# Decoder step with PEER experts: the samples' depthwise convolution on GpSimd, a later place for the second dense group's transposes, and two tile places moved

## The chip, the cores and the metric

The kernel runs on one core of one Trainium2 chip. The metric is the device time of one execution in microseconds (us). In the text PE is TensorE, DVE is VectorE, ACT is ScalarE, POOL is GpSimd and SP is SyncE, which here only starts DMAs. L277 means line 277 of the kernel before, as the profile names it. In the changed kernel most lines from 418 to 736 stand one lower, those from 742 to 884 one higher and those behind up to three higher; the rows of its instruction order carry its own numbers.

## The reference

One layer of a hybrid decoder is applied to 512 prompt tokens and to 32 new tokens of eight sequences (four each, the samples). Each token (1024 values) is projected to retention (queries, keys, values, gate) and to a convolution branch. Retention keeps a 128 x 128 state for each head and sequence. The convolution branch is a gated linear unit and then a causal depthwise convolution over 31 taps, with the last 30 rows of a cache ahead of the samples:

```python
u = ca * jax.nn.sigmoid(cg)
xpad = jnp.concatenate([buf, u], axis=1)
y = conv(xpad, dw_kernel) + dw_bias          # 31 taps, each channel by itself
y = silu(layer_norm(y, ln_g, ln_b))
```

Both branches go through an output projection, are added to the input and normalized to x1. Then PEER: eight heads score x1's queries against two sets of 128 keys, take the best 16 of the sums, and so choose 16 of 16,384 experts for each head and token. Expert e adds `gate * gelu(u_e . x1) * v_e`. A last normalization gives the output. New states and caches are outputs too.

## The kernel before

The 544 tokens are four groups in the expert stage: the first 128 prompt tokens (x1_0, experts gathered by index tile I), the 32 samples (Is), 128 more prompt tokens (Ib), and 256 prompt tokens whose experts are computed densely: all 128 x 128 experts are multiplied with x1 (L884), and a sparse gate matrix is built to weight the products. Those 256 are two dense groups of 128 (`DG`).

The stages, by the profile's times: From 0 to 100 us the first 128 prompt tokens and the samples go through projection (L209), convolution, retention, output projection (L503) and normalization; for the samples the convolution `conv_s` is 62 instructions of 128 x 128 elements: L286 and L287 for the first tap and the bias, then a product into `tap_s` (L290) and an addition (L291) for each of 30 taps. From 91 to 111 the first queries are made (L209, copied by ACT's L753), scored (L545, copied by L547), and the best taken on DVE. From 111 on POOL issues gathers (L628, 1 MB each), and DVE works on each with L634 (dot product), ACT with L645 and L646 (gelu, gate), DVE with L651 (sum). This gather stream is woven into all that follows up to about 734.

From 130 to 412 the other 416 tokens go the same way. Half of their convolution is done on PE (L270) with diagonal matrices that ACT writes (L269); between them stands `retain_s`, the samples' retention: the states of two sequences at a time are loaded (L395), multiplied (L424), updated (L431 on PE, L433 on DVE) and written back (L437). The first pair has a place of its own, `states`, loaded in front on ACT's queue; pairs 2 and 4 lie in the two halves of the tile that also holds the keys; the last pair takes `states` again, loaded on SP's queue after the first has been written back. L785 copies the samples' convolution (`samples`) to the other tokens' (`blk`); L816 loads the samples' x into a place named `xr0`, which held the first tokens' x before.

From 413 to 650 queries, key scores and retrieval for the other groups run, with dense products L884 between them (`early_keys`). Then each dense group's indices are split into row and column numbers on DVE (L919 to L925), transposed by PE (L928), copied by ACT (L932 to L936) and split into two halves on DVE (L938, L940). With these `first_keys` builds gate rows from 684 to 912: M (L989) and B (L993) on DVE, A on ACT and DVE (L978, L985, L986), multiplied on PE (L1009), applied on DVE (L1038) and ACT. From 912 the second dense products (L1066), the last builds, the samples' and the third group's gathers and the end follow.

The order on each engine is set by a scheduler that plays the program through before it is built; `behind(a, b)` makes only the order (a is placed after b), `await_` a wait. Tiles come from pools; a tile that takes the place of another waits for the last use of that one. Each engine works its queue in order, and a waiting instruction holds all that stand behind it.

Of the kernel before, what the change touches and what calls it, by code (L numbers as in the profile page):

```python
# [21 lines left out]
D = 1024  # L22
# [16 lines left out]
FREE = 30  # L39
TB_AT = (30, 34, 56, 80)  # L40
SECOND = 34
TURN = 88
EG = (32, 20, 44, 32)
E0S = (0, 32, 52, 96)

# [53 lines left out]
def tile_step(ctx: ExitStack, tc: tile.TileContext, a, o):  # L99
# [180 lines left out]
    def conv_s(y, after):  # L280

        yp = y.rearrange("p m (b i) -> p m b i", b=SB)
        for k in range(CK):
            w = dw[:, :, k].unsqueeze(2).unsqueeze(3).to_broadcast([128, 4, SB, SQ])
            if k == 0:
                behind(V.tensor_tensor(yp, u_s[:, :, :, 0:SQ], w, op=OP.mult), after)  # L286
                V.tensor_tensor(y, y, dwb.unsqueeze(2).to_broadcast([128, 4, NS]), op=OP.add)  # L287
                continue
            t = small("tap_s", [128, 4, SB, SQ], bufs=1)
            V.tensor_tensor(t, u_s[:, :, :, k:k + SQ], w, op=OP.mult)  # L290
            V.tensor_add(yp, yp, t)  # L291

    def conv_norm(y, n):

# [99 lines left out]
    def load_states(b, r0, q=nc.scalar):  # L394
        return q.dma_start(r0, a["state_retention"][0, b:b + 2].rearrange("b h d e -> d b h e"))  # L395

    def retain_s(qT, kT, v, gT):
# [12 lines left out]
                     start=(h == 0), stop=False, skip_group_check=True)  # L410
        yield
        room = keys_or_scratch()
        rooms = [states, room[:, 0:D], room[:, D:], states]
        for b in range(0, SB, 2):
            r0 = rooms[b // 2].rearrange("p (b h e) -> p b h e", b=2, h=H)
            vx = [small("on", [128, 512]) for _ in range(2)]
            for j in range(2):
                S.activation(vx[j][:n], v[:n], AF.Copy, scale=cc("blk")[:n, b + j:b + j + 1])
            if b:
                load_states(b, r0, nc.sync)  # L420
            for h in range(H):
                for j in range(2):
                    cs = h * n + (b + j) * SQ
                    T.matmul(po[:, cs:cs + SQ], r0[:, j, h], qT[:, h, (b + j) * SQ:(b + j + 1) * SQ],  # L424
                             start=False, stop=(h == H - 1 and b + j == SB - 1), skip_group_check=True)
                if h % 2:
                    yield
            for h in range(H):
                pk = mmps()[:, 0:256]
                for j in range(2):  # L430
                    T.matmul(pk[:, j * DH:(j + 1) * DH], kt[:n, h * DH:(h + 1) * DH], vx[j][:n, h * DH:(h + 1) * DH],  # L431
                             start=True, stop=True)
                V.scalar_tensor_tensor(r0[:, :, h], r0[:, :, h], float(GAMMA[h] ** SQ),  # L433
                                       pk.rearrange("p (b e) -> p b e", b=2), op0=OP.mult, op1=OP.add)
                if h % 2:
                    yield
            nc.sync.dma_start(o[4][0, b:b + 2].rearrange("b h d e -> d b h e"), r0)  # L437
# [299 lines left out]

    advance(0, k_tokens(k0, 0, C, "p"), v0)
    states = fe.tile([128, D], F32, name="states")
    behind(load_states(0, states.rearrange("p (b h e) -> p b h e", b=2, h=H)), lastk)  # L740
    xT = per.tile([128, 8, n], F32, name="x1T")
    nc.scalar.dma_start(xT[:, :, NS:], xt_v[:, :, 160:])
    x1T, xT = xT, xT[:, :, NS:]
# [114 lines left out]
    left = ExitStack()  # L858
    rp = left.enter_context(tc.tile_pool(name="rp", bufs=1, reuse_waits="tile"))
    sel[0] = left.enter_context(tc.tile_pool(name="sel", bufs=2))  # L860
    leftp = ExitStack()
    pq = leftp.enter_context(tc.tile_pool(name="pq", bufs=4, space=PSUM, reuse_waits="tile"))
    psp = [leftp.enter_context(tc.tile_pool(name="psp", bufs=4, space=PSUM, reuse_waits="tile"))]

    banks[:] = [pq]
    load_keys(pool=rp)
    ln2 = [bc_row("lng", a["ln2_g"], D), bc_row("lnb", a["ln2_b"], D)]

    def places(e, ne):
# [20 lines left out]
    qs = {}  # L890
    q_at = lambda c0, w: lambda h, s: qs[h // 2][:, h % 2 * 2 + s, c0:c0 + w]
    DG = ((0, 128), (128, ND - 128))

    for h0 in range(0, PH, 2):
        w = load_w(a["w_query"], h0 * 256)
        qs[h0 // 2] = rp.tile([128, 4, n], F32, name="qs", bufs=2)
        for m in range(4):
            S.activation(qs[h0 // 2][:, m], project(w, m, x1T, 0, n), AF.Copy)
        for h in (h0, h0 + 1):
            key_scores([(h, lambda s: q_at(NS, 128)(h, s))], sb[:, h])  # L900
        p0 = h0 % 4 * NS
        key_scores([(h, lambda s, h=h: q_at(0, NS)(h, s)) for h in (h0, h0 + 1)], ss_[p0:p0 + 2 * NS, h0 // 4], p0)
        if h0 % 4:
            for g, (c0, m) in enumerate(DG):
                retrieve(fresh(q_at(NG2 + c0, m)), range(h0 - 2, h0 + 2), m, eg[:, g], eg[:, 2 + g], h0 - 2)
# [6 lines left out]
            S.activation(places(e, 2), sp, AF.Gelu)  # L912
        return mm

    turned = early_keys(E0S[2], TURN)
    for g, (c0, m) in enumerate(DG):
        ef = eg[:m, g].rearrange("p h k -> p (h k)")
        ei = rp.tile([128, 128], I32, name="ei")[:m]
# [7 lines left out]
        p = mmps().rearrange("p (q t) -> p q t", q=4)  # L926
        for q, t in enumerate((e1, e2, eg[:m, 2 + g].rearrange("p h k -> p (h k)"))):
            mm = T.transpose(p[:, q, :m], t, ident[:m, :m])  # L928
            if g == q == 0:
                behind(mm, turned)  # L930
        gr = rp.tile([128, 128], F32, name="e2")[:, :m]
        S.activation(gr, p[:, 2, :m], AF.Copy, scale=GS)  # L932
        cs = slice(c0, c0 + m)
# [12 lines left out]

    w_, r_ = GSP["s"]
    topk_of("s", lambda h: ss_[:, h], 0, PH // r_, 128)
    early_keys(TURN, E0S[3])
    gbs = ExitStack()  # L950
    gb = gbs.enter_context(tc.tile_pool(name="gb", bufs=1, side="right", reuse_waits="tile"))
    GW[0] = gb.tile([128, EG[0], ND], F32, name="Gb")
# [258 lines left out]
```

## Time and profile before

| | us |
|---|---|
| timed runs (three) | 1500.69, 1508.7, 1509.43; median 1508.7 |
| profiled execution | 1498.04 |
| its span on the core | 1496.3, granted clock 0.988 |
| PE busy | 1437.5 (96%) |
| DVE busy | 1206.1 (81%) |
| ACT busy | 486.6 (33%) |
| POOL busy | 410.3 (27%) |

How it is read: busy time counts an engine's instructions but not waiting and not the issue of DMAs by a queue. PE records twice each product of two float32 tiles. A row of the timeline gives start, length, engine, line and operation, what is written from what, sizes and, in brackets, the idle time ahead of it with what ended it; rows with a count are runs of the same instruction. The waits list, for an engine and line, which engine or DMA ended the idle time ahead of it: total, times, the longest. The chain is followed back from the last instruction to what released each step.

### The profile page before, as it was taken

What the parts mean: (1) busy time and instruction counts of PE and PEld (TensorE: products, weight loads), DVE (VectorE), ACT (ScalarE), POOL (GpSimd) and SP (SyncE); (2) the same over time, 40 slices, a digit from 0 to 9 for tenths busy, and PEclk for the clock granted to TensorE, in tenths of its full rate; (3) what the DMA queues carried; (4) which work ended last, traced back from release to release, by engine and by line L of the source; (5) the groups of instructions that cost most, each with busy time, mean ns of one, the idle gap of its engine ahead of it and who ended that gap; (6) DMA issues with size and microseconds to landing.
All of it is one profiled execution on the core that took longest, in us unless ns stands there. A gap on an engine that the chain in (4) does not pass through costs nothing.

```text
span 1496.3 us, 19303 instructions
## 1 busy us (share of the span) xinstructions
PE 1437.5 (96%) x6486; PEld 981.9 (66%) x6486; DVE 1206.1 (81%) x2977; ACT 486.6 (33%) x1492; POOL 410.3 (27%) x329
## 2 busy tenths in 40 slices
PE   8899989999999999989989999997999999999998
PEld 7877667567857678878878875443454666666443
DVE  4979899997747999998789997677989866666666
ACT  1424452345112322235445543112673111111110
POOL 1002534432323222222222220333333422222330
PEclk9999999999999999999999999998999999999999
DMA  9759678984799789999999985999899999999995
GB/s 345 296 196 409 227 269 280 390 340 155 289 401 369 253 295 348 338 345 355 315 355 343 336 293 173 345 423 416 336 370 391 409 412 410 410 402 406 409 415 194
DMA packets 99536, 503.60 MB, mean 337 GB/s; under 512 B 10183, under 2 KB 21191, under 8 KB 56549
## 3 DMA queue, kind: packets, MB, share of 16 engines
q0 software_dynamic: 42240, 305.12, 52.6%
q1 hardware_dynamic: 53197, 190.61, 33.8%
q10 hardware_dynamic: 4000, 6.64, 1.3%
q8 instruction: 51, 0.84, 0.2%
q14 instruction: 48, 0.39, 0.1%
HBM read 496.96 MB, written 5.80 MB: 336 GB/s over the span
## 4 chain that ended last, share of the span: by engine, by line
PE 40%; DVE 28%; DMA 21%; issue 9%; POOL 2%; ACT 1%; DVEq 0%; SPq 0%; POOLq 0%; ACTq 0%
PE pB L1066 17%; PE sp L884 14%; DMA g<-in_uv_dram,I 8%; DMA g<-in_uv_dram,Ib 7%; DVE acc L651 6%; DVE g L634 6%; DMA g<-in_uv_dram,Is 3%; PE mm L209 3%; POOL g L628 2%; DVE g L277 2%; PE mm L503 1%; PE mm L1009 1%; PE mm L270 1%; PE mm L318 1%; DVE iu L533 1%
## 5 line engine op out<-in xcount | busy, mean ns | idle before, releaser
L884 PE MATMUL sp<-x1T,uv 128*128 128x256 f32 x2048 | 464.1, 383 | 0.9 <-ACT Gc L1024 0.5
L634 DVE SCALAR_TENSOR_TENSOR g<-g,x 128x1024 f32<-128x1024 f32 x288 | 350.1, 1217 | 107.6 <-DMA g<-in_uv_dram,I 50.0
L884 PEld LDWEIGHTS sp<-x1T,uv 128*128 128x128 f32 x2048 | 385.8, 191 | 67.6 <-issue 14.0
L651 DVE SCALAR_TENSOR_TENSOR acc<-g,wgt,acc 128x1024 f32<-128x1024 f32 x285 | 364.2, 1278 | 66.3 <-ACT wgt L646 65.4
L628 POOL DMA_INDIRECT g<-in_uv_dram,I x128 | 185.5, 1449 | 423.2 <-DVE acc L651 242.3
L645 ACT ACTIVATE act<-act 128x1 f32<-128x1 f32 x288 | 58.0, 201 | 621.0 <-DVE g L634 620.6
L628 POOL DMA_INDIRECT g<-in_uv_dram,Ib x128 | 160.0, 1250 | 359.7 <-PE pB L1066 125.2
L209 PE MATMUL mm<-x1T,w 128*128 128x384 f32 (+1 forms) x512 | 177.0, 504 | 0.0
L1066 PE MATMUL pB<-uv,Ga 128*128 128x512 f32 x352 | 158.4, 596 | 0.0
L209 PEld LDWEIGHTS mm<-x1T,w 128*128 128x128 f32 x512 | 97.3, 192 | 72.8 <-issue 40.7
L1066 PEld LDWEIGHTS pB<-uv,Ga 128*128 128x128 f32 x352 | 65.7, 190 | 69.6 <-issue 66.5
L1066 PE MATMUL pB<-uv,Gb 128*128 128x512 f32 x256 | 111.4, 594 | 0.0
L1066 PE MATMUL pB<-uv,Gd 128*128 128x512 f32 x256 | 110.0, 592 | 0.0
L1066 PEld LDWEIGHTS pB<-uv,Gd 128*128 128x128 f32 x256 | 48.6, 190 | 60.8 <-issue 59.5
L1066 PEld LDWEIGHTS pB<-uv,Gb 128*128 128x128 f32 x256 | 48.2, 190 | 61.2 <-issue 55.7
L628 POOL DMA_INDIRECT g<-in_uv_dram,Is x32 | 41.3, 1289 | 149.0 <-DVE acc L651 30.9
L985 ACT ACTIVATE off<-row,e1T 128x128 bf16<-128x128 bf16 x256 | 78.9, 393 | 4.1 <-PE mm L1009 3.7
L1066 PE MATMUL pB<-uv,Gc 128*128 128x512 f32 x160 | 74.5, 611 | 0.7 <-DMA uv<-in_uv_dram 0.6
L1009 PEld LDWEIGHTS <-A 128*128 128x128 f16 x1024 | 43.4, 97 | 41.1 <-issue 22.4
L1022 ACT ACTIVATE W<-sp 128x256 f32<-128x256 f32 (+26 forms) x84 | 26.8, 319 | 124.1 <-PE sp L884 106.5
L209 PE MATMUL mm<-g,w 128*128 128x160 f32 (+1 forms) x512 | 65.4, 287 | 0.0
L209 PEld LDWEIGHTS mm<-g,w 128*128 128x128 f32 x512 | 64.4, 191 | 0.7
(287 smaller groups left out, 1595.3 us busy)
## 6 DMA issues: line engine op xcount, KB each, us to landing
uv<-in_ut_dram SPq DMA_DIRECT2D x128, 512.0 KB
uv<-in_uv_dram SPq DMA_DIRECT2D x128, 512.0 KB
w<-in_w_in_dram SPq DMA_DIRECT2D x18, 1024.0 KB
w<-in_w_query_dram SPq DMA_DIRECT2D x16, 1024.0 KB
w<-in_w_out_dram SPq DMA_DIRECT2D x7, 1024.0 KB
g<-in_uv_dram,I POOLq DMA_INDIRECT x128, 8.4
g<-in_uv_dram,Ib POOLq DMA_INDIRECT x128, 9.6
x1T<-in_xT_dram ACTq DMA_DIRECT2D x1, 1536.0 KB
```

Source lines behind the costliest of these rows:

```text
L209: T.matmul(p[:, :n], w[m // 2][:, k, (m % 2) * 128:(m % 2 + 1) * 128], xT[:, k, c0:c0 + n], start=(k == 0), stop=(k == 7))
L270: T.matmul(p[:, :L], dg[:, k % 4], u_p[:, m, p0 + k:p0 + k + L], start=(k == 0), stop=(k == CK - 1))
L277: V.scalar_tensor_tensor(y[:, m], u_p[:, m, p0 + k:p0 + k + L], dw[:, m, k:k + 1], y[:, m], op0=OP.mult, op1=OP.add)
L628: fetch = G.indirect_dma_start(out=t, out_offset=None, in_=a["uv"], in_offset=bass.IndirectOffsetOnAxis(ap=idx[:, k:k + 1], axis=0))
L634: dot = V.scalar_tensor_tensor(t[:, :D], t[:, :D], 1.0, x1, op0=OP.mult, op1=OP.mult, accum_out=act[:, 0:1])
L645: S.activation(act[:, 1:2], act[:, 0:1], AF.Gelu)
L651: V.scalar_tensor_tensor(acc, v, wgt, acc, op0=OP.mult, op1=OP.add)
L884: mm = T.matmul(sp[:, i], u[:, k], x1T[:, k, NG2:], start=(k == 0), stop=(k == 7), skip_group_check=True)
L985: S.activation(off[:, t], row, AF.Abs, bias=e1T[:, t1 + t:t1 + t + 1])
L1009: mm = T.matmul(pt[:, t % nt], A[t % TB], B[:, q, t % TB // 2, :, t % 2], start=(q == 0), stop=(q == 1))
L1022: S.activation(W[:, :n], sp[:, :n], AF.Gelu)
L1066: return [T.matmul(pB[b][q], W[:, b * 128:(b + 1) * 128], vt[:, q * 512:(q + 1) * 512], start=False, stop=(e == NK - 1), skip_group_check= ...
```

## The change

There are four edits.

1. `conv_s` issues all its 62 instructions on POOL (`G`) instead of DVE (`V`).
2. `early_keys` for keys 52 up to 94 is called twice ahead of the dense groups: up to 88 and from 88 to 94. The first transpose of group 0 is ordered behind the first call, that of group 1 behind the second. Before, one call went up to 88, group 1's had no order of its own, and the rest of the keys up to 96 came later.
3. `retain_s` takes the pairs in the order 0, 6, 2, 4. Pair 6 has a place `states6`, a tile named `xr0`, loaded in front on ACT's queue with pair 0; only 2 and 4 are loaded by SP inside the loop.
4. The queries of the other groups (`qs`) and the keys lie in a new pool `rk`, opened after the retrieval's `sel`, and the first `qs` is placed ahead of the keys. So the build rows, whose tiles come after this region is closed, lie over queries and keys and no longer over the retrieval's tiles.

```diff
-TURN = 88
+TURN = (88, 94)
...
     def conv_s(y, after):
...
-                behind(V.tensor_tensor(yp, u_s[:, :, :, 0:SQ], w, op=OP.mult), after)
-                V.tensor_tensor(y, y, dwb.unsqueeze(2).to_broadcast([128, 4, NS]), op=OP.add)
+                behind(G.tensor_tensor(yp, u_s[:, :, :, 0:SQ], w, op=OP.mult), after)
+                G.tensor_tensor(y, y, dwb.unsqueeze(2).to_broadcast([128, 4, NS]), op=OP.add)
...
-            V.tensor_tensor(t, u_s[:, :, :, k:k + SQ], w, op=OP.mult)
-            V.tensor_add(yp, yp, t)
+            G.tensor_tensor(t, u_s[:, :, :, k:k + SQ], w, op=OP.mult)
+            G.tensor_add(yp, yp, t)
...
-        rooms = [states, room[:, 0:D], room[:, D:], states]
-        for b in range(0, SB, 2):
-            r0 = rooms[b // 2].rearrange("p (b h e) -> p b h e", b=2, h=H)
+        for b, place in ((0, states), (6, states6), (2, room[:, 0:D]), (4, room[:, D:])):
+            r0 = place.rearrange("p (b h e) -> p b h e", b=2, h=H)
...
-            if b:
+            if b in (2, 4):
                 load_states(b, r0, nc.sync)
...
-    behind(load_states(0, states.rearrange("p (b h e) -> p b h e", b=2, h=H)), lastk)
+    states6 = fe.tile([128, D], F32, name="xr0")
+    for b, place in ((0, states), (6, states6)):
+        behind(load_states(b, place.rearrange("p (b h e) -> p b h e", b=2, h=H)), lastk)
...
+    rk = left.enter_context(tc.tile_pool(name="rk", bufs=1, reuse_waits="tile"))
...
-    load_keys(pool=rp)
...
+    qs[0] = rk.tile([128, 4, n], F32, name="qs", bufs=2)
+    load_keys(pool=rk)
...
-        qs[h0 // 2] = rp.tile([128, 4, n], F32, name="qs", bufs=2)
+        qs[h0 // 2] = qs[0] if h0 == 0 else rk.tile([128, 4, n], F32, name="qs", bufs=2)
...
-    turned = early_keys(E0S[2], TURN)
+    turned = [early_keys(*x) for x in ((E0S[2], TURN[0]), TURN)]
...
-            if g == q == 0:
-                behind(mm, turned)
+            if q == 0:
+                behind(mm, turned[g])
...
-    early_keys(TURN, E0S[3])
+    early_keys(TURN[1], E0S[3])
```

**POOL, at about 67 to 111 us.** Before, POOL did only two reciprocal roots here, each an addition (L194) and a power (L195): `hrs` for the heads' normalization, `lrs` for the layer normalization that gives x1_0. Then come the gathers.

```order
L194 TENSOR_SCALAR hrs_621<-hrs_621 128x4 [waits DVE_49]
L195 TENSOR_TENSOR hrs_621<-hrs_621,mhalf_102 128x4 [waits Pool_49]
L194 TENSOR_SCALAR lrs_717<-lmv_713 128x1 [waits DVE_49]
L195 TENSOR_TENSOR lrs_717<-lrs_717,mhalf_102 128x1 [waits Pool_49]
L628 DMA g_2581<-in_uv_dram,I0_114 128x2048 [waits DVE_49,DMASW0_49,PE_49,Activation_49]
```

In the changed kernel one product (L290) stands ahead of the loads in front, 41 of the convolution's instructions stand between `hrs` and `lrs`, and one more inside `lrs`:

```order
L291 TENSOR_TENSOR samples_127<-samples_127,tap_s_1314 128x128 [waits Pool_49]
L290 TENSOR_TENSOR tap_s_1317<-u_s_108,cols_90 128x128 [waits Pool_49]
L291 TENSOR_TENSOR samples_127<-samples_127,tap_s_1317 128x128 [waits Pool_49]
L194 TENSOR_SCALAR lrs_717<-lmv_713 128x1 [waits DVE_49]
L290 TENSOR_TENSOR tap_s_1320<-u_s_108,cols_90 128x128 [waits Pool_49]
L195 TENSOR_TENSOR lrs_717<-lrs_717,mhalf_102 128x1 [waits Pool_49]
L291 TENSOR_TENSOR samples_127<-samples_127,tap_s_1320 128x128 [waits Pool_49]
```

Behind these stand 18 more and then the gathers. Each waits for POOL's one before. On ACT the copy of the result (L785) keeps its place between the first and the second copy of the first queries (L753), and waits for POOL's last convolution instruction instead of DVE's.

**ACT, at about 211 to 223 us.** The rows are diagonals for PE (L269), a gather's gelu and gate (L644 and L645 there, L645 and L646 before), and the load of the samples' x, which before stood in front at 85.5 us, where the load of pair 6 now stands.

```order
L269 ACTIVATE dg<-cst_89,cols 128x128 [waits PE_49]
L269 ACTIVATE dg<-cst_89,cols 128x128 x3
L817 DMA xr_2268<-in_x_dram 32x1024 [waits DMAHW5_49,DMAHW4_49,DVE_49]
L644 ACTIVATE act<-act 128x1 [waits DVE_49]
L645 ACTIVATE wgt<-act,GT_113 128x1 [waits Activation_49]
L269 ACTIVATE dg<-cst_89,cols 128x128 [waits PE_49]
```

The load now waits for the write-back of pair 6 from the same place (DMAHW4), which SP issues after the pair's last update on DVE.

**PE, at about 650 to 684 us.** Dense products (L884) around the transposes of the second dense group (L928), before:

```order
L884 MATMUL sp<-x1T,uv 128x256 x2
L928 MATMUL mm<-cst_89,e_4129 128x128 [waits DVE_49]
L884 MATMUL sp<-x1T,uv 128x256 x5
L884 MATMUL sp<-x1T,uv 128x256 [waits DMAHW6_49]
L884 MATMUL sp<-x1T,uv 128x256 x4
L928 MATMUL mm<-cst_89,e_4131 128x128 [waits DVE_49]
L928 MATMUL mm<-cst_89,eg 128x128
```

In the changed kernel, where the two lines are L885 and L931:

```order
L885 MATMUL sp<-x1T,uv 128x256 [waits DMAHW0_49]
L885 MATMUL sp<-x1T,uv 128x256 x7
L931 MATMUL mm<-cst_89,e_4199 128x128 [waits DVE_49]
L931 MATMUL mm<-cst_89,e_4201 128x128 [waits DVE_49]
L931 MATMUL mm<-cst_89,eg 128x128
L885 MATMUL sp<-x1T,uv 128x256 [waits DMAHW1_49,Activation_49]
```

From the first group's transposes to the second group's first one stand 19 products before and 48 now; 16 follow up to the first L1009 now, 37 before.

More of the change, by code (lines that the diff above doesn't have):

```diff
@@ L424, in retain_s @@
                     T.matmul(po[:, cs:cs + SQ], r0[:, j, h], qT[:, h, (b + j) * SQ:(b + j + 1) * SQ],
-                             start=False, stop=(h == H - 1 and b + j == SB - 1), skip_group_check=True)
+                             start=False, stop=(h == H - 1 and b + j == 5), skip_group_check=True)
                 if h % 2:
```

## The prediction

> **What bounds the kernel now.** I read the page's head first, then PE's waits, then the timelines at the places that the change touches. Start with the busy times.
>
> ```profile
> span 1496.3 us, 19303 instructions
> PE 1437.5 (96%) x6486; PEld 981.9 (66%) x6486; DVE 1206.1 (81%) x2977; ACT 486.6 (33%) x1492; POOL 410.3 (27%) x329
> ```
>
> PE is busy in all but 58.8 us of the span, so a gain must come out of those 58.8, and every new stall of PE is lost time unless DVE would have stopped PE a little later anyway. PE's waits, longest first (us in total, times, longest):
>
> ```profile
> PE mm L1009 <- DVE Ga L1038: 8.9, 7, 1.7
> PE mm L1009 <- DVE B L993: 8.9, 2, 6.3
> ...
> PE mm L928 <- DVE e L922: 6.6, 1, 6.6
> ...
> PE mm L424 <- DMA states<-in_state_retention_dram: 2.7, 1, 2.7
> ```
>
> The change aims at two of these rows: 6.6 (second dense group's transposes) and 2.7 (last states). The rest, the two DVE rows of L1009 above all, is not touched directly. The profiled execution took 1498.04 us, 1.7 more than its span. The three timed runs have a median of 1508.7, so the span is 0.8% below it; my sum is a difference against the profiled execution, carried over to the runs at the end.
>
> **The samples' convolution on POOL.** First what its 62 instructions cost on DVE and whether they are in anyone's way there (count, busy us, mean ns):
>
> ```profile
> L291 DVE TENSOR_TENSOR samples<-samples,tap_s 128x128 f32<-128x128 f32 x30 | 8.7, 291 | 0.9
> L290 DVE TENSOR_TENSOR tap_s<-u_s,cols 128x128 f32<-128x128 f32 x30 | 8.7, 290 | 0.8
> L532 DVE MAX8 vf<-score 128x8 f32<-128x128 f32 x4 | 1.0, 282 | 5.6 <-ACT score L547 5.6
> ```
>
> With L286 and L287 that is 18 us, but after it DVE stands still for 5.6 us until a score arrives, and DVE's path instructions in this stretch begin when PE releases them:
>
> ```profile
> 82.85 1.89 PE L503 MATMUL mm<-w,g 128*128 128x256 f32 x8
> 84.78 0.69 DVE L732 SCALAR_TENSOR_TENSOR x<-xr,mm 128x512 f32<-128x512 f32 x1
> 88.15 3.62 PE L318 MATMUL mm<-x1T,g 128*32 128x256 f32 x16
> 88.23 1.41 DVE L485 SCALAR_TENSOR_TENSOR x<-x,lrs,lnb 128x512 f32<-128x512 f32 x2
> 91.70 0.66 PE L514 MATMUL mm<-cst,x 128*128 128x128 f32 x4
> ```
>
> L732 starts 0.04 after L503's end; L485 ends at 89.64, and its reader L514 waits for PE's own L318 until 91.70. So I put the 18 us freed on DVE at nothing: PE's L503 and L318 hide them.
>
> On POOL the same instructions are a chain, each waiting for the one before, and two things now stand behind them: the second normalization's rsqrt (lrs) behind 41 of them, and ACT's L785 behind all 61 that come after hrs. POOL's rows, from the timeline, from the groups (mean ns of one behind the bar), and of L195 all lrs together (minimum/median/maximum ns):
>
> ```profile
> 67.39 0.23 POOL L194 TENSOR_SCALAR hrs<-hrs 128x4 f32<-128x4 f32 x1 [15.29 <-DVE hrs L335]
> 67.71 1.06 POOL L195 TENSOR_TENSOR hrs<-hrs,mhalf 128x4 f32<-128x4 f32 x1
> 86.67 0.23 POOL L194 TENSOR_SCALAR lrs<-lmv 128x1 f32<-128x1 f32 x1 [17.90 <-DVE lmv L472]
> 86.98 0.90 POOL L195 TENSOR_TENSOR lrs<-lrs,mhalf 128x1 f32<-128x1 f32 x1
> ...
> L201 POOL MEMSET u_p<- 128x120 f32 x1 | 0.2, 190 | 0.0
> L188 POOL MEMSET mhalf<- 128x1 f32 x1 | 0.1, 90 | 0.0
> ...
> L195 POOL TENSOR_TENSOR lrs<-lrs,mhalf x7: 568/584/1562, 87.0 to 938.1; 128x1 f32<-128x1 f32 x5, 32x1 f32<-32x1 f32 x2
> ```
>
> A 128x128 tensor_tensor on POOL is not in the trace. Bounds for the step d from one to the next, with the 0.08 us that lie between dependent POOL rows (67.62 to 67.71): not under 0.23 + 0.08 = 0.31, the smallest arithmetic row; not over 1.06 + 0.08 = 1.14, four elements of a power. I take the plain L194, since mult and add are plain, and add the length: the memset grows by 0.10 us from 1 to 120 elements, and two inputs and an output are three such streams: 0.23 + 0.30 + 0.08 = 0.61. The 128x1 power took 0.90 at 86.98 beside DVE's L480, 0.32 over its median; I add that for the four two-input halves of L480 and L485: 1.3 us in all.
>
> [...]
>
> Now what waits. These are ACT's and PE's rows there:
>
> ```profile
> 97.19 0.30 ACT L785 ACTIVATE blk<-samples 128x128 f32<-128x128 f32 x1
> 97.91 0.28 ACT L753 ACTIVATE qe<-mm 128x128 f32<-128x128 f32 x1 [0.42 <-PE mm L209]
> 101.65 0.39 PE L545 MATMUL mm<-keys,qe 128*128 128x128 f32 x2
> 111.21 1.12 POOL L628 DMA_INDIRECT g<-in_uv_dram,I  x1 [23.33 <-DVE iu L533]
> ```
>
> The chain starts when hrs ends, 68.8. First branch: lrs ends at 68.8 + 42d + 0.3 + 0.9, half of L485 (0.7) later L514 can run: 70.7 + 42d against 91.70 + 0.07, a loss above d = 0.50. Second: the last conv instruction ends at 68.8 + 61d + 1.3 for the two rsqrt instructions; then L785 0.30, L753 0.28 and the gaps, 0.8 together: L545 starts at 70.9 + 61d against 101.65, a loss above d = 0.504. The second is later, and holds the first score, the indices and the first gather at 111.21. Behind L545 PE has the same queue as before, and the gathers begin later by as much, so I see no place that returns it. Loss: 61 x (0.61 - 0.504) = 6.5, plus 1.3. Bounds: 0 to 61 x (1.14 - 0.504) = 38.8.
>
> **The fourth state pair's place.** Gain first, then the new wait. From the chain the two transfers, then PE's, DVE's and ACT's timelines:
>
> ```profile
> 197.50 7.35 DMA out_dram<-states
> 204.91 9.98 DMA states<-in_state_retention_dram
> ...
> 203.23 3.18 PE L318 MATMUL mm<-w,x1T 128*128 128x256 f32 x14
> 207.63 1.15 PE L431 MATMUL mm<-on,ktok 32*128 32x128 f32 x8
> 208.72 3.49 PE L270 MATMUL mm<-u_p,dg 128*128 128x384 f32 x10
> 214.94 3.15 PE L424 MATMUL mm<-samples,states 128*128 128x4 f32 x14 [2.73 <-DMA states<-in_state_retention_dram]
> ...
> 214.85 0.74 DVE L433 SCALAR_TENSOR_TENSOR keys<-keys,mm 128x256 f32<-128x256 f32 x2
> ...
> 218.65 0.20 ACT L645 ACTIVATE act<-act 128x1 f32<-128x1 f32 x1 [2.52 <-DVE g L634]
> 222.72 1.28 ACT L269 ACTIVATE dg<-cst,cols 128x128 f32<-128x128 f32 x4 [3.54 <-PE mm L270]
> ```
>
> Write-back and reload stand one behind the other and cost PE 2.73; the reload is gone, so 2.7 gained. But the place is xr0's, which the samples' x (L816) takes next: its load now waits on ACT's queue for the write-back of that place. The second pair's last update stays at about 215.6 (the keys' pair in that place ends there); with 7.35 for the write-back ACT is held until 223.0, and behind it stand L645, L646 for the gather's sum and L269's diagonals for PE's convolution. Diagonals come at about 224.2 (issue 0.34, L645 0.2, L646 0.3, one diagonal 0.32). What PE has until it needs them: from the 207.63 on four L431 products, six convolution products L270, five of L318 (0.23 a record), two L431, four L270, four L431, four L270, four L318. The trace counts each product twice, so by the rows 10 x 0.29 + 14 x 0.70 + 9 x 0.45 = 16.8, to 224.4. So PE just makes it; if the write-back takes 9.98 as the load of equal size did, PE stalls 2.4, and DVE's L651 comes 2.4 late even so, as ACT's L646 is held to 223.8. I take 1.0 between 0 and 2.4: net gain 1.7.
>
> **The second group's transposes.** PE's rows around them:
>
> ```profile
> 650.80 8.37 PE L884 MATMUL sp<-x1T,uv 128*128 128x256 f32 x38
> 665.79 0.47 PE L928 MATMUL mm<-cst,e 128*128 128x128 f32 x1 [6.62 <-DVE e L922]
> 672.02 11.82 PE L884 MATMUL sp<-x1T,uv 128*128 128x256 f32 x54
> 683.68 0.55 PE L1009 MATMUL mm<-B,A 128*128 128x96 f16 x9
> 754.69 0.52 PE L1009 MATMUL mm<-B,A 128*128 128x96 f16 x8 [1.39 <-DVE Ga L1038]
> 890.89 1.05 PE L1009 MATMUL mm<-B,A 128*128 128x96 f16 x16 [1.50 <-DVE Ga L1038]
> ```
>
> Between the two groups' transposes now stand 96 of these products instead of 38. 58 more x 0.217 (11.82 / 54) are 12.6 us, more than 6.62: the stall goes. What is late next: PE does all behind it 6.6 us earlier (its first L1009, with eight products more ahead of it, at 683.68 - 6.62 + 16 x 0.217 = 680.5), and so comes earlier to each L1038 that it waits for between 754.69 and 890.89. There DVE sets the pace, and its order brings those L1038 forward by one or two gather steps (an L634 and an L651 each) at the first and by nothing at the last. So PE arrives early and waits longer; I keep 1.0 of the 6.6, less than one of those stalls, bounds 0 and 6.6.
>
> **Build rows over keys and queries.** The first build row on DVE stands four gather steps earlier, before the second group's L922. PE has L884 to do then, and nothing waits for a build row before the first L1009, so I put it at 0; without that cover a build row would be one more stall like the 1.39 at 754.69.
>
> **Sum:** 6.5 + 1.3 - 2.7 + 1.0 - 1.0 = +5.1 us: 1503.1 for a run like the profiled one.
>
> **The rivals.** *Slower, one mechanism:* the fixed part of a two-input POOL instruction decides. The power took 1.06 for four elements and 0.58 for one, 0.16 an element, so 0.42 is fixed; with the 0.30 for length and 0.08 between, d = 0.80. Then POOL's chain ends 18.1 late, total 18.1 + 1.3 - 2.7 + 1.0 - 1.0 = +16.7, 1525. For it: the same form of instruction; against: the power may have a fixed part of its own. It decides over 1% from d = 0.77 on. *Gains kept:* d under 0.50 and the write-back at 7.35, so nothing is late in front, and the builds on DVE follow PE: -2.7 - 6.6 = -9.3, 1499.4. For it: DVE has 18 us less; against: these lie in its pauses in front, and the seven waits for L1038 say that DVE can't follow. *The moves cancel:* d near 0.5, and DVE swallows the transposes' gain and the states': 0, 1509.
>
> **How the numbers follow.** My forecast 0.47 (from -2 to +14), the slow chain 0.27, the gains kept 0.12, the cancelling 0.14. About 1% (15 us) is what a measurement of this kernel can tell from no change. Faster by over 1%: 0.11, as even all gains together give 0.6%, so a part must be one that I don't see. Slower by over 1%: the slow chain and the top of the forecast, 0.29. Within 1%: 0.60. The four executions shown are two at 1498 and 1501 and two at 1509; their middle is 1504.7, the runs' median 1508.7. With +5.1 these give 1509.8 and 1513.8; I say 1512. The range goes from 1496, all gains from the middle, to 1530, the slow chain with the 3 us more at its top; my forecast's own is 1503 to 1523.
>
> **What would show it.** Right: POOL's 62 rows at about 0.53 us, one each 0.61, the last near 107; ACT's L785 right behind it, and an idle time of PE of 6 to 8 us at the second L545, near 101; the first gather at 118 to 119; no wait for states at 215, but ACT idle before L816's load until about 223 and a stall of PE of at most 2.4 us at L270; no wait of L928 at 665, and more wait of L1009 for L1038 than 8.9. Wrong, if POOL's step is under 0.50 or over 0.77, if L1009's waits stay at 8.9 (then the 6.6 was kept), or if L634 waits less for its gathers than before and returns the front's loss.

## The result and the profile after

The changed kernel is faster by 9.5 us in the median: 1499.11 us (1494.58 to 1506.49, 17 runs) against 1508.59 (1500.69 to 1518.81, 17 runs of the kernel before), a ratio of 0.9933 [0.9917, 0.995]. The prediction had +5.1 us and 1512. The number that came is that of its rival "gains kept", 1499.4, which had a chance of 0.12. That this number fits is in part luck: its 9.3 us count 2.7 for the states, which the runs below can't tell from nothing, and no half clock, which they show. One run of the kernel before, slow at 1534.05 us and a granted clock of 0.942, is left out of all that follows.

The first profiled execution of the changed kernel took 1503.62 us (span 1501.7), near the upper end of its runs; that of the kernel before, 1498.04, lies below all its timed runs. So this pair of profiles goes the other way than the runs, and a second profile of each was taken (below). No sum over whole spans is read from one pair here.

The head and PE's waits of the changed kernel's first profile (its L931, L1012, L1041 are L928, L1009, L1038 of the kernel before; us in total, times, longest):

```profile
span 1501.7 us, 19301 instructions
PE 1440.7 (96%) x6486; PEld 981.0 (65%) x6486; DVE 1191.2 (79%) x2915; ACT 484.5 (32%) x1492; POOL 436.8 (29%) x391
...
PE mm L1012 <- DVE Ga L1041: 11.3, 9, 2.4
...
PE mm L1012 <- DVE B L996: 5.6, 2, 3.1
```

The waits of 6.6 for the second group's transposes and of 2.7 for the states have left the head of the list. The wait for the gate products' readers went from 8.9 to 11.3, by 2.4 and not by the 5.6 that the prediction let it take back. POOL's groups from 60 to 110 us (count, then busy us, mean ns) and places in its timeline and PE's:

```profile
L291 POOL TENSOR_TENSOR samples<-samples,tap_s 128x128 f32<-128x128 f32 x30 | 14.6, 488 | 2.3
L290 POOL TENSOR_TENSOR tap_s<-u_s,cols 128x128 f32<-128x128 f32 x29 | 12.7, 439 | 2.2
```

```profile
68.55 0.40 POOL L286 TENSOR_TENSOR samples<-u_s,cols 128x128 f32<-128x128 f32 x1
...
86.19 0.97 POOL L291 TENSOR_TENSOR samples<-samples,tap_s 128x128 f32<-128x128 f32 x1
87.24 0.74 POOL L290 TENSOR_TENSOR tap_s<-u_s,cols 128x128 f32<-128x128 f32 x1
...
101.56 0.46 POOL L291 TENSOR_TENSOR samples<-samples,tap_s 128x128 f32<-128x128 f32 x1
112.32 1.13 POOL L627 DMA_INDIRECT g<-in_uv_dram,I  x1 [10.31 <-DVE iu L532]
```

```profile
92.71 0.66 PE L513 MATMUL mm<-cst,x 128*128 128x128 f32 x4 [1.32 <-DVE x L484]
...
102.05 0.31 ACT L786 ACTIVATE blk<-samples 128x128 f32<-128x128 f32 x1 [3.62 <-POOL samples L291]
```

A step of the chain is 0.49 to 0.54 us (100.03, 100.53, 101.07, 101.56 at its end), not 0.61. ACT's copy waits 3.62 for it, as predicted, but at 102.05 and not near 107, and PE has no wait at its second key scores (L544, at 102.79), where 6 to 8 us were forecast. The first gather is issued at 112.32 against 111.21: 1.1 us late, not 7.8. Nearly all of it comes by the other branch, the second normalization: PE's L513 waits 1.32 for it and starts at 92.71 after 91.70. In the second profile PE waits at neither place.

PE at the second group's transposes:

```profile
659.70 13.54 PE L885 MATMUL sp<-x1T,uv 128*128 128x256 f32 x62
673.08 0.27 PE L931 MATMUL mm<-cst,e 128*128 128x128 f32 x1
674.37 0.33 PE L931 MATMUL mm<-cst,e 128*128 128x128 f32 x1 [1.02 <-DVE e L928]
...
674.65 7.07 PE L885 MATMUL sp<-x1T,uv 128*128 128x256 f32 x32
682.14 0.85 PE L1012 MATMUL mm<-B,A 128*128 128x96 f16 x16 [0.41 <-ACT e2T L939]
682.83 3.68 PE L885 MATMUL sp<-x1T,uv 128*128 128x256 f32 x16
```

The wait of 6.62 is 1.02 here, and there is none in the second profile. The records also show a loss that the prediction had not priced. The kernel before by stretches (length; busy us of PE, PEld, DVE, ACT, POOL with counts; granted PE clock, DMA share, GB/s):

```profile
207.00:215.00 8.00, 5.27 (x22) 2.92 (x20) 8.00 (x15) 3.42 (x11) 3.04 (x2) 1.00 0.97 334
215.00:222.00 7.00, 7.00 (x21) 5.24 (x22) 6.18 (x11) 1.62 (x6) 1.07 (x1) 0.51 0.98 327
222.00:226.00 4.00, 4.00 (x20) 2.79 (x19) 3.16 (x7) 1.82 (x7) 1.07 (x1) 1.00 0.40 119
658.00:662.00 4.00, 1.17 (x6) 0.69 (x4) 4.00 (x11) 1.65 (x7) 1.01 (x1) 1.00 0.98 385
662.00:669.00 7.00, 3.21 (x9) 2.63 (x10) 7.00 (x17) 0.98 (x3) 2.72 (x2) 0.51 0.85 340
669.00:672.00 3.00, 3.00 (x16) 2.62 (x15) 2.63 (x6) 0.50 (x2) 0.18 (x1) 1.00 0.98 337
```

From the waits of 2.73 and 6.62 on, PE's granted clock is 0.51 for about 7 us. Behind the first, PE is busy all the time and loses about half, 3.4 us. The second stretch begins inside the wait, so only the 3.21 us of work in it are slowed, by about 1.6. In the changed kernel the place of the transposes has the full clock:

```profile
666.00:674.00 8.00, 7.35 (x35) 6.18 (x33) 8.00 (x16) 4.10 (x13) 1.21 (x1) 1.00 0.90 352
674.00:680.00 6.00, 5.63 (x27) 5.01 (x28) 5.49 (x11) 0.98 (x3) 2.18 (x2) 1.00 0.98 365
```

### The profile page after: what moved, and what is told of

Its sections match the earlier page's. It is cut to its first block, busy times and chain, and to the rows that moved or that the text cites. A ratio compares the mean times of both kernels' runs of the same rounds, so it can differ in the third digit from the quotient of the medians.

```text
span 1501.7 us, 19301 instructions
## 1 busy us (share of the span) xinstructions
PE 1440.7 (96%) x6486; PEld 981.0 (65%) x6486; DVE 1191.2 (79%) x2915; ACT 484.5 (32%) x1492; POOL 436.8 (29%) x391
## 4 chain that ended last, share of the span: by engine, by line
PE 49%; DVE 21%; DMA 19%; issue 6%; POOL 3%; ACT 2%; DVEq 0%; SPq 0%; POOLq 0%; ACTq 0%
PE pB L1069 21%; PE sp L885 14%; DMA g<-in_uv_dram,I 7%; PE mm L209 7%; DMA g<-in_uv_dram,Ib 5%; DVE acc L650 5%; DMA g<-in_uv_dram,Is 4%; DVE g L633 4%; DVE g L277 2%; DMA uv<-in_ut_dram 2%; PE mm L270 2%; PE mm L318 1%; POOL g L627 1%; PE mm L1012 1%; DVE B L996 1%
## 5 line engine op out<-in xcount | busy, mean ns | idle before, releaser
L885 PE MATMUL sp<-x1T,uv 128*128 128x256 f32 x2048 | 466.3, 383 | 3.2 <-ACT Gb L1027 1.3
L885 PEld LDWEIGHTS sp<-x1T,uv 128*128 128x128 f32 x2048 | 385.6, 191 | 71.2 <-issue 15.6
L627 POOL DMA_INDIRECT g<-in_uv_dram,I x128 | 180.6, 1411 | 417.7 <-DVE acc L650 271.2
L644 ACT ACTIVATE act<-act 128x1 f32<-128x1 f32 x288 | 58.0, 201 | 637.2 <-DVE g L633 632.6
L1012 PEld LDWEIGHTS <-A 128*128 128x128 f16 x1024 | 43.8, 97 | 41.3 <-issue 22.0
L1012 PE MATMUL mm<-B,A 128*128 128x96 f16 (+1 forms) x1024 | 47.9, 191 | 17.6 <-DVE Ga L1041 11.3
```

The source lines that it names most:

```text
L627: fetch = G.indirect_dma_start(out=t, out_offset=None, in_=a["uv"], in_offset=bass.IndirectOffsetOnAxis(ap=idx[:, k:k + 1], axis=0))
L644: S.activation(act[:, 1:2], act[:, 0:1], AF.Gelu)
L885: mm = T.matmul(sp[:, i], u[:, k], x1T[:, k, NG2:], start=(k == 0), stop=(k == 7), skip_group_check=True)
L1012: mm = T.matmul(pt[:, t % nt], A[t % TB], B[:, q, t % TB // 2, :, t % 2], start=(q == 0), stop=(q == 1))
```

## The experiments

After the result four causes stood against each other. **Hand-over:** the gain lies near 650 to 690 us, where PE passes from dense products (L884) to gate products (L1009): enough products must stand ahead of each instruction that waits there. **DVE relieved:** the 18 us of convolution that left DVE are what counts. **States:** the reload's wait and what follows it. **Place:** the build rows over other tiles, and with them another order of gate products and their readers up to 912 us. In all edits below the rest of the kernel is as named, and every kernel computes the whole reference.

### One edit at a time

`e1_only_conv` is the kernel before with edit 1 (the four lines with `V` to `G` in `conv_s`), `e2_only_states` with edit 3 (`states6`), `e3_only_turn` with edit 2 (`TURN = (88, 94)`), `e4_only_rk` with edit 4 (pool `rk`).

```diff
-            V.tensor_tensor(t, u_s[:, :, :, k:k + SQ], w, op=OP.mult)
+            G.tensor_tensor(t, u_s[:, :, :, k:k + SQ], w, op=OP.mult)
```

> Kernel before with the first edit alone: the samples' convolution on POOL. Stall theory (the gain came from PE's waits of 2.73 at 214.94 and 6.62 at 665.79, each with a stretch of half PE clock behind it): those waits stay, and the front loses the 1.1 us that the changed kernel's first gather came later, so +1 us, ratio 1.000 to 1.002, no gain. Freed-DVE theory (the 18 us taken off DVE are what helped): 5 to 9 us faster, ratio 0.994 to 0.997.

Measured 1.0028 [1.001, 1.0047], median 1510.92: alone, the convolution's move makes the kernel slower, though by little; by the mean spans (2.0 ± 2.7 us) no difference can be told.

```diff
-        rooms = [states, room[:, 0:D], room[:, D:], states]
+        for b, place in ((0, states), (6, states6), (2, room[:, 0:D]), (4, room[:, D:])):
```

> Kernel before with the third edit alone: the last pair of states in a place of its own. Stall theory with the clock: the 2.73 us wait and the 8 us of half clock from 214 to 222 (3.4 us lost) go, so 3 to 6 us faster, ratio 0.996 to 0.998. Wait-only theory: at most 2.7 faster, 0.998 or nearer to 1. Freed-DVE theory: no gain, 1.000.

Measured 0.9994 [0.9967, 1.0021], median 1507.4: no difference that can be told.

```diff
-    turned = early_keys(E0S[2], TURN)
+    turned = [early_keys(*x) for x in ((E0S[2], TURN[0]), TURN)]
```

> Kernel before with the second edit alone: the second dense group's transposes behind 96 more products. Stall theory with the clock: the 6.62 us wait goes and with it half clock from 665.8 to 669, 8.3 us in all; what of it stays behind the waits for L1038 is 3 to 8 us, ratio 0.995 to 0.998. Swallowed (my prediction's step): 0 to 1 us, 0.999 to 1.000, with the waits of L1009 for L1038 grown by about 6. Freed-DVE theory: 1.000.

Measured 1.0008 [0.9983, 1.0033], median 1509.79. The transposes no longer wait, and the waits of L1009 for L1038 have not grown by 6 but fallen to 5.5; but a wait has come in the transposes' place (PE's timeline of this kernel):

```profile
677.40 7.07 PE L884 MATMUL sp<-x1T,uv 128*128 128x256 f32 x32
688.92 1.46 PE L1009 MATMUL mm<-B,A 128*128 128x96 f16 x16 [4.45 <-ACT A L986]
690.19 5.42 PE L884 MATMUL sp<-x1T,uv 128*128 128x256 f32 x16
```

The gate product's operand A is late by 4.45 us, since without edit 4 its build rows stand later; and the 16 records behind it take 5.42 us instead of the 3.68 they take in the changed kernel.

```diff
-    load_keys(pool=rp)
+    load_keys(pool=rk)
```

> Kernel before with the fourth edit alone: queries and keys in their own pool, so that the build rows lie over them. Stall theory: 0 alone, ratio 0.999 to 1.001. Place theory (the earlier build rows carry the gain, as DVE is the bound from 680 to 890): 3 us or more faster, 0.998 or under, with less wait of L1009 for L1038 than the 8.9 us before.

Measured 0.9968 [0.9945, 0.9991], median 1501.4: the only single edit that gains. It doesn't do so at the hand-over. PE's waits from 640 to 950 us in its trace:

```profile
PE mm L930 <- DVE e L924: 6.5, 1, 6.5
PE sp L884 <- ACT Gc L1026: 1.9, 3, 1.1
PE mm L1011 <- DVE Ga L1040: 0.8, 1, 0.8
```

The wait for the second group's transposes is as long as before (6.5 after 6.6). What has gone is the wait of the gate products for their readers, 0.8 after 8.9, as the place cause says. The four ratios together make -0.02%, the four edits together -0.67%: by the ratios they act on one another.

### All but one

The changed kernel with one edit undone: `f1_no_conv` (the convolution on DVE again), `f2_no_states`, `f3_no_turn`, `f4_no_rk`; the diffs are those above, reversed.

> The changed kernel with the samples' convolution back on DVE. If the edits add up (alone it cost 0.28%), the rest gains more: ratio to the kernel before 0.989 to 0.992. If the 18 us taken off DVE help once the build rows and transposes are moved: 0.996 or over.

Measured 1.0003 [0.9982, 1.0023], median 1507.07. Without the convolution on POOL nothing is left of the gain. That is what "DVE relieved" says, but the trace shows something else. PE's timeline of this kernel:

```profile
675.50 0.59 PE L931 MATMUL mm<-cst,e 128*128 128x128 f32 x2
...
676.04 3.62 PE L885 MATMUL sp<-x1T,uv 128*128 128x256 f32 x16
685.24 0.88 PE L1012 MATMUL mm<-B,A 128*128 128x96 f16 x9 [5.59 <-ACT e2T L939]
685.92 5.69 PE L885 MATMUL sp<-x1T,uv 128*128 128x256 f32 x16
```

Here 16 records (8 products) stand between the last transpose and the first gate product, where the changed kernel has 32. So PE arrives 3.5 us sooner, and what it needs, the transposes' copies on ACT, stands behind a gather's gelu:

```profile
683.51 0.20 ACT L644 ACTIVATE act<-act 128x1 f32<-128x1 f32 x1 [3.59 <-DVE g L633]
...
684.89 0.30 ACT L939 ACTIVATE e2T<-mm 128x128 f16<-128x128 f32 x1
```

PE waits 5.59, and again the 16 records behind take 5.69. The scheduler's order here had changed with the engine of a convolution that ends at 102 us. It changed further on too: from the 32 records of L490 (L489 here) near 690 us to about 1150, PE's order in this kernel is that of the kernel before, row for row, and not that of the changed kernel.

> The changed kernel with the last states' reload as before. If the edits add up (alone it gave 0.06%): 0.993 to 0.995. Stall theory with the clock (2.7 and 3.4 us come back): 0.996 to 0.998.

Measured 0.995 [0.9924, 0.9975], median 1502.83: most of the gain without the states' edit.

> The changed kernel with the second group's transposes where they stood before. If the edits add up (alone it cost 0.08%): 0.992 to 0.994, and the wait of L928 for L922 of some 6 us is back in the trace. If later transposes and earlier build rows work only together: 0.997 or over.

Measured 0.9982 [0.996, 1.0004], median 1504.11: most of the gain goes without the transposes' edit. In its trace the second group's first transpose waits 2.92 at 667.47, and the next 32 records take 8.77 instead of 7.07.

> The changed kernel with queries and keys in the old pool, so that the build rows lie over the retrieval's tiles. Place theory (alone it gave 0.32%): 1.000 to 1.003, all gain gone, and PE waits 4 us or more for the first A or B in front of its first gate products. If it adds only its own 0.32%: 0.996 to 0.997.

Measured 0.9946 [0.9921, 0.997], median 1499.69. The pool `rk`, the one edit that gains alone, can be left out. The order gives a likely reason: here 22 products stand ahead of the first gate product, PE's wait for A is 3.4 instead of the 4.45 of e3, in this trace no half clock follows it, and the order behind it is another than e3's.

### The order held, the convolution on DVE

To tell the order from the engine, `g1_no_conv_held` is f1 with one more line of order, which puts all 16 products ahead of the first gate product again. `g2_turn_rk_held` is the kernel before with edits 2 and 4 and that line: convolution on DVE, states as before.

```diff
-    early_keys(TURN[1], E0S[3])
+    early_last = early_keys(TURN[1], E0S[3])
...
+                    if t == q == 0 and not ahead:
+                        behind(mm, early_last)
```

> The changed kernel with the samples' convolution on DVE, and one order added: the first gate product (L1012) stands behind the last early dense product, so that 16 products and not 8 lie between the second group's transposes and it, as in the changed kernel. Hand-over theory (the gain is PE's way from the dense products to the gate products at 650 to 690 without a long wait; POOL matters only because it turned the scheduler to that order): the gain comes back with the convolution on DVE, ratio 0.993 to 0.996, and the wait for e2T falls from 5.6 to 3 us or less. Freed-DVE theory: as without the order, 0.999 to 1.002.

Measured 0.9934 [0.9907, 0.9961], median 1501.04. With the convolution on DVE and the order of the changed kernel at this one place the whole gain is back:

```profile
680.71 7.07 PE L885 MATMUL sp<-x1T,uv 128*128 128x256 f32 x32
688.84 0.85 PE L1012 MATMUL mm<-B,A 128*128 128x96 f16 x16 [1.06 <-ACT e2T L939]
689.52 3.68 PE L885 MATMUL sp<-x1T,uv 128*128 128x256 f32 x16
```

The wait of 5.59 is 1.06, and the records behind it run at 3.68. "DVE relieved" falls: 0.9934 with the 18 us on DVE and 0.9933 without (f1 and g1 come from different series, each against its own runs of the kernel before).

But the line did not change this place alone. From L490 on, PE's order in g1 is neither that of f1 nor that of the changed kernel: but for its first rows it is that of e4. The wait of the gate products for their readers, 8.2 in f1 and 11.3 in the changed kernel, is 0.3 here, and near 1047 us stands one long wait in place of those for B (as in e4, 10.0):

```profile
PE mm L1012 <- ACT act L644: 11.0, 1, 11.0
```

So g1 shows that the gain needs no convolution on POOL. It can't show that the hand-over alone makes it.

> The kernel before with the second and fourth edit and that same order, the convolution on DVE and the states as before. Hand-over theory: most of the gain without the other two edits, ratio 0.994 to 0.997. Freed-DVE theory: 0.999 to 1.002. If the states are part of it, 0.996 to 0.998.

Measured 0.9943 [0.9917, 0.997], median 1501.18: two edits and one line of order make the gain, within the interval, without the convolution's move and without the states'. From L490 on, its order is g1's.

### Two more profiles, and one try at the rest

`p1_before` and `p2_after` are the two kernels as they are, for a trace alone.

> The kernel before once more, for its trace alone. If the first profiled execution was a lucky one (half clock in 214 to 222, 412 to 417, 569 to 574, 662 to 669 and 1037 to 1048 only, where every single-edit kernel also had it near 70), the span is 1500 or more here and half clock shows near 70. If not, 1496 to 1498 again.

Span 1511.7, granted clock 0.982.

```profile
PE mm L424 <- DMA states<-in_state_retention_dram: 9.4, 1, 9.4
PE mm L1009 <- DVE Ga L1038: 9.2, 5, 2.7
...
PE mm L928 <- DVE e L922: 6.2, 1, 6.2
```

The transposes' wait is there again (6.2 after 6.6). The states' wait is not a constant: 9.4 here and 2.7 in the first profile, since the reload itself took 16.68 us after 9.98.

> The changed kernel once more, for its trace alone. If the first profiled execution was an unlucky one, the span is 1495 to 1500; the wait of L931 and e2T at 650 to 690 stays under 2 us in either case by the hand-over theory.

Span 1497.6. The transposes don't wait at all, no half clock stands between 640 and 950, and the gate products' row is nearly that of the other profile:

```profile
PE mm L1012 <- DVE Ga L1041: 11.5, 10, 2.0
```

`h1_paced` is the changed kernel with eight second dense products ordered between the last gate products' units near 1040 us, where PE waits for B (5.6 in the first profile of the changed kernel, 8.4 in the second).

```diff
+                    if ahead and q == 0 and t % nt == 0 and t:
+                        behind(mm, marks[-1])
```

> The changed kernel with one order added: each unit of 32 of the last gate products stands behind the second products issued by then, so that eight products of L1069 lie between two units and not four or fewer. If a long wait of PE costs its length and the half clock behind it, also outside the hand-over, then the waits for B near 1040 (5.6 to 8.4 us, 5.1 us lost to the clock) shrink by 3 us or more and the ratio is 0.988 to 0.992. If DVE's order holds the last stage whatever PE does, the waits only move and the ratio stays 0.992 to 0.995.

Measured 0.9944 [0.9917, 0.9971], median 1502.26. The waits for B are 5.9, in four pieces and not two, between the 5.6 and the 8.4 of the changed kernel's traces: most of them were moved. No gain over it can be told, and whether this place can be mended stays open.

### Waits and clock over all runs

Every timed run lists its span and its mean granted clock. Clock lost is (1 - clock) x span; what is left of the span is work at full clock and PE's waits. The split is rough: half clock inside PE's own waits or behind its last product counts as clock lost, though it slows no work; in the single traces that is 3 to 10 us of 15 to 28. Means of each kernel's runs less those of the kernel before in the same series, with about 95% (two standard errors); the changed kernel's 17 runs against 88 of the kernel before from the series of e, f and g (the row of before gives their means themselves; against one series alone the changed kernel gains 8.0 to 12.0 us). Ahead of them the order near 650 to 690 us (S48 is 48 dense products, T3 three transposes, G gate products; the first T3 is the first group's), the order from L490 on (A is that of the kernel before, B that of the changed kernel, C that of g1) and, from one trace each, PE's waits plus clock lost from 640 to 950 us.

| kernel | order near 650 to 690 | from L490 on | 640 to 950: waits + clock lost | clock lost, all runs | rest, all runs |
|---|---|---|---|---|---|
| before | S40 T3 S19 T1 S10 T2 S27 G9 | A | 16.0 + 3.4; p1: 17.6 + 10.2 | 21.6 | 1485.8 |
| changed | S40 T3 S48 T3 S16 G16 | B | 14.8 + 3.4; p2: 13.0 + 0 | -4.2 ± 1.4 | -5.5 ± 1.5 |
| e1 | S40 T3 S16 T1 S11 T2 S21 G14 | own | 17.8 + 5.1 | +2.0 ± 1.9 | 0.0 ± 2.3 |
| e2 | as before | A | 14.1 + 3.4 | -0.1 ± 2.0 | -1.0 ± 2.3 |
| e3 | as changed | A, but for its first rows | 10.8 + 5.1 | +0.2 ± 1.9 | +0.2 ± 2.8 |
| e4 | S40 T3 S20 T1 S12 T2 S16 G5 | C, but for its first rows | 10.0 + 3.4 | -1.4 ± 1.6 | -4.6 ± 2.8 |
| f1 | S40 T3 S48 T3 S8 G9 | A | 17.1 + 6.8 | -1.1 ± 1.7 | +0.8 ± 2.5 |
| f2 | as changed | B | 12.7 + 3.4 | -2.1 ± 2.0 | -3.9 ± 2.7 |
| f3 | S40 T3 S16 T1 S16 T2 S16 G1 | own | 11.1 + 3.4 | +1.5 ± 1.9 | -4.6 ± 2.1 |
| f4 | S40 T3 S48 T3 S22 G13 | own | 12.5 + 0 | -1.8 ± 2.6 | -6.3 ± 2.1 |
| g1 | as changed | C | 5.6 + 3.4 | -4.9 ± 1.9 | -5.2 ± 2.5 |
| g2 | as changed | C | 11.2 + 0 | -6.6 ± 1.9 | -3.2 ± 2.4 |
| h1 | as changed | B up to 950 | 16.7 + 0 | -2.5 ± 2.4 | -6.1 ± 3.7 |

The changed kernel's 9.7 us of mean span are, by this split, 5.5 of waits and work and 4.2 of half clock. What e1 costs stands, by the means, in the clock column. f3 has the smaller rest but no gain in clock, f1 and e3 have neither. By the single traces, the seven kernels at 0.9968 or less (e4, f2, f4, g1, g2, h1 and the changed one, its two traces averaged) have 13.5 us of waits and clock lost between 640 and 950 on average, the six at 0.998 or more (before, its two traces averaged, e1, e2, e3, f1, f3) 19.7; without the half clock inside the waits it is 13.2 and 18.6. Their mean ratios, 0.9945 and 1.0003, are 8.6 us apart. One trace of a kernel is a weak witness here, as the two of before (19.4 and 27.8) show, and h1 (16.7) gains with more than e3 (15.9), which doesn't.

Two things separate the kernels that gain, and the runs don't part them. At the transposes and the first gate product, the changed kernel, f2, g1, g2 and h1 wait at most 2.4 us at a time, the kernel before, e1, e2, e3 and f1 from 4.4 to 6.6; f3 and f4 stand between them with 2.9 and 3.4. And from L490 on, no kernel with order A gains. e4 has the long wait at the hand-over (6.5) and another order behind it, and gains about half by its ratio, so the later order seems worth something by itself. A kernel with the changed kernel's hand-over and all of order A behind it was not run; e3, the nearest, has the wait of 4.45 for A.

## Why the prediction was wrong, step by step

**The step that failed: "There DVE sets the pace ... So PE arrives early and waits longer; I keep 1.0 of the 6.6."** The transposes' stall went as predicted, but the gate products' waits took back 2.4 (8.9 to 11.3, and 9.2 to 11.5 in the second profiles), not 5.6. It is one of two terms that failed; the other, the convolution's 6.5 + 1.3 further below, was the larger miss in us and gave the sum its sign: without it the same sum is -2.7. That PE waits for DVE seven times didn't say that DVE sets the pace; DVE's own waits in the same stretch (640 to 950 us), which I had not read, say otherwise. In the kernel before and in the changed one:

```profile
DVE Gb L1038 <- PE mm L1009: 13.7, 6, 5.0
```

```profile
DVE Gb L1041 <- PE mm L1012: 14.0, 6, 4.5
```

DVE stands still for 13.7 us for PE's gate products, and PE for 8.9 for DVE's readers of them. Each waits for the other in turn, so a stall ahead of the whole stretch need not be slack of the other engine. The order of the stretch changed as well, and in e4, g1 and g2 the same wait is 0.8, 0.3 and 3.5: its length hangs on the order more than the prediction allowed. The text named its own sign, L1009's waits staying at 8.9; they stayed nearer to it than to the forecast.

**The price of a wait was its length alone.** The prediction's "a gain must come out of those 58.8" left out that PE's busy time holds work at half clock too. By the rough split above that is some 4 of the 9.7 us. The rows to see it stood in the prediction: L424 x14 took 3.15 after the wait of 2.73, and in the changed kernel, where the state pair's wait is gone, x12 take 1.40 (PE's timeline):

```profile
202.30 1.40 PE L423 MATMUL mm<-samples,keys 128*128 128x4 f32 x12
```

**The convolution on POOL, +6.5: right in kind, the step mis-sized.** I had 0.61, measured about 0.51 (0.42 and 0.46 plus 0.07 between), on the very edge of 0.504 from which a loss began; 1.1 us late at the first gather where 7.8 was forecast, and no wait of PE for it in the second profile. The length was the term in error: over the 0.23 of the plain row it adds 0.19 to 0.23, not 0.30, and the pause between rows is 0.07. The branch was wrong too: the second normalization made PE late, not the copy on ACT. The 18 us freed on DVE bring nothing, as predicted (g1 against the changed kernel). e1 alone is slower by 0.28%, about 4 us, by its ratio and by 2.0 ± 2.7 by its mean span; whether that is more than the 1.1, and through which waits, was not settled.

The 1.3 for the instructions beside DVE's two-input halves was right in size. Beside DVE's L479 and L484 four rows of POOL take 0.74 to 0.97 (two of them above) against 0.46 and 0.42 otherwise, 1.5 us more in all; why they are longer there was not shown. By their means the 128 x 128 rows take 439 ns on POOL and 290 on DVE (product), 488 and 291 (addition): 1.5 and 1.7 times as long. The range's top of 1530 has 3 us more for the slow chain, a term that no run shows: a step took about 0.51 and not that chain's 0.80, and those four rows 1.5 us more in all.

**The states, -2.7 + 1.0.** The wait is gone. The new wait of the samples' x on ACT is there too, issued at 219.42 instead of 223, and no PE wait follows from it. What this is worth can't be told: e2, f2 against the changed kernel and g2 against g1 give 0.06 to 0.17%, each inside its interval, though p1 shows that the wait can be 9.4.

**Build rows, 0.** This term was put at nothing, and not rightly: alone it gains 0.32% (e4), as the gate products' waits for their readers go from 8.9 to 0.8. At the first gate product too: e3 waits 4.45 for A, and edit 4 brings the rows forward. In f4, without it, six more products ahead leave a wait of 3.4, and the whole gain is there all the same.

**What the order change meant.** I read the numbers of products ahead of the transposes and of the first gate product in the order, but took the second as a consequence. It decides whether PE waits there: with 8 products (f1) it waits 5.59 for the copies on ACT; with 16 (7.0 us) it waits 0 to 2.4 where edit 4 is in. That one line of order at that place brings the gain back in g1 is shown by the run; that it does so at that place alone is not, since the order from L490 on changed with it. That the scheduler's choice of 8, and of order A behind it, came from the convolution's engine is what f1 and the changed kernel differ by.

**What stays open:** How the gain divides between the hand-over and the order behind it. In front, a wait of PE for DVE's L226 at 300 to 305 us is 0 in both traces of before, 4.3 and 1.1 in the changed kernel's, and 0.4 to 6.7 in the others; part of the gain in front may be given back there. It was not tried.

## What to carry to other kernels

Before a stall's gain is written off because "the other engine sets the pace", read that engine's own waits in the same stretch: if it waits back, part of the gain may stay, as 4.2 of the 6.6 did here in the waits. Where a scheduler decides the order, an edit far away can move the instruction that matters; undo each edit both alone and from the whole, and then hold the order at the suspected place with one line, which told here an engine's move (worth nothing) from an order (worth 10 us). Then compare the rest of the order as well: here the line changed it up to 1150 us at least, and the place was not isolated. And add to the price of a PE wait of 2.5 us or more the clock behind it: half clock stood within 4 us behind 70 of 78 such waits here, and 3.4 us of it cost f3 1.7 us of work.

## What the runs showed of the hardware

**Half clock after a wait.** In 14 traces (all but h1's) PE's granted clock falls to 0.50 in or after a wait, mostly for 3.4 or 6.8 us; work that falls into it loses half, at most 1.7 or 3.4 (in f3, with the clock at 0.50 from about 667.8 to 671.3, the 32 records behind the wait of 2.92 took 8.77 us instead of 7.07). Half clock stood within 4 us behind PE waits of 4 us and more 21 times of 21, of 3 to 4 us 27 of 30, of 2.5 to 3 us 22 of 27 (in 11 of these the half clock of an earlier wait was still running), of 2 to 2.5 us 13 of 27, of 1.5 to 2 us 5 of 20, of 1 to 1.5 us 10 of 72. Without the 11, it stood behind waits of 2 to 3 us 24 times of 43; why behind some and not behind others was not shown. The wait of 6.7 to 6.9 us at the start of each span, ahead of PE's first work, is not among them; no half clock followed it.

**Runs differ by it.** In the 88 runs of the kernel before, the mean span is 1511.3 us below a granted clock of 0.9845 (26 runs) and 1504.3 from 0.9865 up (29 runs): a part of the spread of 21 us between runs (1498.89 to 1519.99) goes with the clock. One way into it is a transfer that is not always equally quick: the states' reload took 9.98 us in one trace and 16.68 in the other. With the wait of 9.4, from 215.0 to 224.4 us, the clock was 0.50 from 217.4 to 231.0; about half of that lies in the wait itself, and the work behind it lost about 3.3 us.
